# Attention scores of a two-layer decoder trunk: float32 products at depth 64 in two halves of the array, in place of stacked float32r parts

## Chip, cores, metric

The kernel runs on one core of a Trainium2 chip. Its engines are TensorE (PE, with its weight loads PEld), VectorE (DVE), ScalarE (ACT), GpSimd (POOL) and SyncE (SP, which issues most transfers). The metric is the device time of one execution in microseconds.

## What is computed

Two residual layers on x of 512 tokens by 1024 channels, float32. Layer 0 mixes tokens by stick-breaking attention (16 heads of 64), layer 1 by dilated window attention (three groups of 8 heads of 64, merged by their softmax denominators). Each is followed by a feed-forward part with a causal convolution of width 3. Cut to what matters here:

```python
# layer 0, per head and block of 128 queries
z = einsum(q, k) * 64 ** -0.5                       # float32
log_not = where(key < query, log_sigmoid(-z), 0)
between = reverse_cumsum(log_not) - log_not
a = where(key < query, exp(log_sigmoid(z) + between), 0)
o = a @ v                                           # then o @ w_o
# layer 1, per group (window, dilation) in ((128, 1), (512, 4), (2048, 16))
s = einsum(q, k) * 64 ** -0.5 + bias(distance)      # inside the window, causal
p = softmax(s);  o_g = p @ v;  o = sum_g softmax(lse)_g * o_g
# after each: x += post_norm(...); x += post_norm(conv_ffn(pre_norm(x)))
```

## The kernel before

Most products run in three passes of float32r: an operand is cast to a high part H, and the rest is a low part L; H by H, H by L and L by H are added (`mm3`, lines 200 to 203). Weights come in chunks of 128 by 1024 through the class `Weights`. `load` issues the transfer, `split` makes H on ScalarE (line 73) and L on VectorE, or on the engine that it is given (line 74), and `done` is called after the last use of a chunk, splits the next and loads one more. Five split chunks are held.

Layer 0 (lines 370 to 583) works on eight pairs of heads. `fill_qk(p)` projects a pair's queries and keys in two chunks, each in two halves of the depth, and yields after each half: four ticks of twelve products of 512 columns per pair. Each chunk ends with `ws.done(nc.gpsimd)`, so the split of the next goes to GpSimd, and with `stack` (lines 347 to 367): VectorE scales the product by 1 / rms of the tokens into a temporary f (line 351). For queries, ScalarE casts one head's half to H (357), VectorE makes L beside it (358). For keys, ScalarE casts H twice (362, 363), VectorE makes L (364) and copies it (367). With H of q above L of q on the 128 partitions, and H or L of k twice, two float32r products of depth 128 make a score.

`scores(p, i)` is for query tile i. It makes the scores of two heads (line 468; 512, 384, 256 and 128 keys for i = 0 to 3), adds the mask (472), takes two sigmoids on ScalarE (476, 477), a running product on VectorE (the scan, 479) and the product b * u (482). Tiles 0 and 1 use one bank of PSUM per head; tiles 2 and 3 hold both heads in one bank, and are masked and taken through the sigmoids for both heads at once. `turn_a(p, j)` transposes on TensorE (498) and evicts on VectorE and ScalarE (503, 507, 508). `values(p)` multiplies by v (517), the two heads in two column halves of the array.

The fillers, the projections of the pairs and then products with the output weights (`fill_o`), set the order: at fixed ticks after them stand the parts of each pair. A pair's scores 0 and 1 are queued behind the first half of the next pair's queries, scores 2 and 3 one tick later, and its last transposes just ahead of the scores 0 and 1 of the next pair:

```python
for dt, f, a in (
    (0, scores, 0), (0, scores, 1), (1, scores, 2), (1, scores, 3),
    (2, turn_a, 0), (3, turn_a, 1), (4, turn_a, 2), (4, turn_a, 3),
):
    at_tick(b + dt, f, p, a)          # b = 4 * p + 5
at_tick(b + 5, values, p)
```

All semaphores, and the order within an engine where the data leave it open, come from the tile framework, which also hands out the eight banks of PSUM.

Layer 1 works on four pairs of heads. Group 0 has its scores by `stack` as above (line 840). Groups 1 and 2 have float32 products of depth 64 and 32 by 128 outputs, at eight places of the array (line 847: two row halves by four column quarters); their queries and keys are scaled only (line 824).

Of the kernel before, what the change touches and what calls it, by code (L numbers as in the profile page):

```python
# [10 lines left out]
F32 = mybir.dt.float32  # L11
F32R = mybir.dt.float32r
# [5 lines left out]
P = 128  # L18
# [21 lines left out]
# Columns of one head's bias table: two key blocks of group 0, then groups 1 and 2.  # L40
# [4 lines left out]
class Weights:  # L45
    """The weights in chunks of [128, 1024], in the order of their use: loaded ahead and split
    into the float32r parts H and L, with H + L the weight to 24 bits."""
# [55 lines left out]
def hybrid_trunk_kernel(  # L103
# [39 lines left out]
    # ---- the order of the weights  # L143
# [30 lines left out]
    # The gains of the norms before the sub-layers, by channel.  # L174
# [17 lines left out]
    # The factors 1 / rms by token.  # L192
# [6 lines left out]
    # ---- products in three passes  # L199
# [5 lines left out]
    def proj_f(o, w, k0, k1, cols=slice(0, S)):  # L205
        """128 features by tokens; the chunk holds all of the depth."""
# [4 lines left out]
    def keep_busy(n):  # L211
        """Products that nothing uses: the clock of TensorE rises after some us of work."""
# [30 lines left out]
    def half_sum(ss, b, a, name):  # L243
        """(a + eps + b) / 2"""
# [28 lines left out]
    def fill_rows(ts, sums, idn, name):  # L273
        """1 / rms of a run of token tiles, in `rows` and one token to a partition."""
# [15 lines left out]
    def post_norm(t, m0, ss0, m1, g, name, last):  # L290
        """m0 has been multiplied by the gain."""
# [18 lines left out]
    class Sub:  # L310
        """The end of a sub-layer: its columns in two halves, the second token tile by token
        tile, each followed by the norms that lead to the next sub-layer."""
# [20 lines left out]
        def square(self, t):  # L333
# [3 lines left out]
            # The token tile waits in DRAM for the sub-layer's end; its place serves it.  # L337
# [721 lines left out]
```

## Time and profile before

| | |
|---|---|
| median of 3 runs | 1335.27 us (1334.65 to 1335.76) |
| span of the profiled execution, first to last instruction | 1333.9 us |
| TensorE busy | 1282.0 us, 96% |
| weight loads | 1045.4 us, 78% |
| VectorE busy | 846.1 us, 63% |
| ScalarE busy | 577.1 us, 43% |
| GpSimd busy | 92.8 us, 7% |
| mean granted TensorE clock | 0.982 of full speed |

The profiled execution's own time is its span, 1333.9 us, and what lies around it at the launch; the runs' median is 1.4 us above the span. Matmuls are pipelined, so each one's time in the trace is longer than the distance to the next, and a busy TensorE is not one at its peak. Shares of the whole span mix stages with different limits. A line such as L74 is line 74 of the kernel.

### The profile page before, as it was taken

The page shows a single profiled execution, that of the slowest core. Times are in us where ns is not written, and L with a number is a line of the kernel's source. Part 1 is how long each engine was busy: PE and PEld are TensorE (multiplying, and loading weights), DVE is VectorE, ACT ScalarE, POOL GpSimd, SP SyncE. Part 2 cuts the span into 40 slices and gives each one's busy share as a digit, 9 for nine tenths or more (in the row PEclk, how much of TensorE's full clock was granted, in tenths as well). Part 3 has the DMA queues.
Part 4 walks back from the last instruction along what each step waited for, and adds up shares of the span by engine and source line. Part 5 has one row for each costly group of instructions (what it writes and reads, how often), then busy time and mean ns, then how long its engine had stood idle before and what let it go on. Part 6 is the DMA issues. An engine that isn't in the chain of part 4 may idle for free.

```text
span 1333.9 us, 17026 instructions
## 1 busy us (share of the span) xinstructions
PE 1282.0 (96%) x6568; PEld 1045.4 (78%) x6568; DVE 846.1 (63%) x1485; ACT 577.1 (43%) x949; POOL 92.8 (7%) x101
## 2 busy tenths in 40 slices
PE   8989898989999999999998999999899999999997
PEld 7866666779888888888866888887698888888886
DVE  5289999677777777423573465674877777773224
ACT  6355555446444444222364443454554444442210
POOL 2032222020000000000210000000200000000000
PEclk8999999999999999999998999999899999999999
DMA  5321112233332233333245253332333333333321
GB/s 205 111 79 38 47 43 95 67 127 119 102 95 95 95 95 128 128 100 96 94 154 115 86 133 86 99 103 75 114 111 96 96 98 104 98 127 126 95 64 63
DMA packets 48464, 133.48 MB, mean 100 GB/s; under 512 B 14239, under 2 KB 16319, under 8 KB 48384
## 3 DMA queue, kind: packets, MB, share of 16 engines
q1 hardware_dynamic: 44176, 118.26, 28.2%
q0 software_dynamic: 4208, 14.14, 3.5%
q8 instruction: 51, 0.84, 0.3%
q14 instruction: 29, 0.24, 0.1%
HBM read 122.78 MB, written 9.60 MB: 99 GB/s over the span
## 4 chain that ended last, share of the span: by engine, by line
PE 76%; DVE 12%; issue 6%; ACT 3%; DMA 2%; POOL 0%; SPq 0%; DVEq 0%; ACTq 0%; POOLq 0%
PE up L201 12%; PE up L202 12%; PE up L203 12%; PE dn L202 6%; PE dn L201 6%; PE dn L203 6%; PE dqk L201 4%; DVE u L479 3%; PE dqk L203 3%; PE dqk L202 3%; DVE b L482 3%; DMA wraw<-in_dl_qk_dram 2%; PE v L203 1%; PE v L202 1%; PE v L201 1%
## 5 line engine op out<-in xcount | busy, mean ns | idle before, releaser
L74 DVE TENSOR_TENSOR wl<-wraw,wh 128x1024 fp32r<-128x1024 f32 x175 | 214.1, 1224 | 207.1 <-ACT wh L73 204.6
L73 ACT CAST wh<-wraw 128x1024 fp32r<-128x1024 f32 x204 | 214.4, 1051 | 267.4 <-PE dn L203 137.8
L201 PE MATMUL up<-hH,wh 128*128 128x512 f32 (+1 forms) x768 | 284.9, 375 | 9.8 <-ACT hH L267 9.8
L202 PE MATMUL up<-hL,wh 128*128 128x512 f32 (+1 forms) x768 | 286.1, 374 | 0.0
L203 PE MATMUL up<-hH,wl 128*128 128x512 f32 (+1 forms) x768 | 285.4, 373 | 0.0
L201 PEld LDWEIGHTS up<-hH,wh 128*128 128x128 f32 x768 | 144.6, 190 | 35.7 <-ACT hH L267 10.3
L202 PEld LDWEIGHTS up<-hL,wh 128*128 128x128 f32 x768 | 145.9, 190 | 25.0 <-DVE hL L268 0.3
L203 PEld LDWEIGHTS up<-hH,wl 128*128 128x128 f32 x768 | 145.8, 190 | 24.9
L202 PE MATMUL dn<-wl,gH 128*128 128x512 f32 x352 | 138.7, 394 | 0.0
L201 PE MATMUL dn<-wh,gH 128*128 128x512 f32 x352 | 138.0, 392 | 0.0
L203 PE MATMUL dn<-wh,gL 128*128 128x512 f32 x352 | 136.6, 388 | 0.0
L607 DVE SCALAR_TENSOR_TENSOR up<-work,cw,up 128x510 f32<-128x510 f32 (+1 forms) x176 | 131.4, 751 | 5.0 <-ACT up L605 2.2
L604 DVE TENSOR_TENSOR work<-up,rows 128x512 f32<-128x512 f32 x88 | 60.1, 687 | 70.6 <-PE up L203 70.3
L201 PEld LDWEIGHTS dn<-wh,gH 128*128 128x128 f32 x352 | 66.1, 188 | 15.4
L74 POOL TENSOR_TENSOR wl<-wraw,wh 128x1024 fp32r<-128x1024 f32 x29 | 71.5, 2472 | 95.0 <-ACT wh L73 94.7
L201 PE MATMUL dqk<-hH,wh 128*128 128x512 f32 x192 | 77.8, 405 | 0.0
L203 PEld LDWEIGHTS dn<-wh,gL 128*128 128x128 f32 x352 | 66.1, 188 | 14.8
L202 PEld LDWEIGHTS dn<-wl,gH 128*128 128x128 f32 x352 | 66.2, 188 | 13.1
L203 PE MATMUL dqk<-hH,wl 128*128 128x512 f32 x192 | 75.1, 391 | 0.0
L202 PE MATMUL dqk<-hL,wh 128*128 128x512 f32 x192 | 75.0, 391 | 0.0
L605 ACT ACTIVATE up<-work,cb,cw 128x512 f32<-128x512 f32 x88 | 68.5, 779 | 11.3 <-DVE work L604 10.9
L618 ACT CAST gH<-work 128x512 fp32r<-128x512 f32 x44 | 27.2, 619 | 106.6 <-DVE work L617 106.6
(251 smaller groups left out, 1897.3 us busy)
## 6 DMA issues: line engine op xcount, KB each, us to landing
wraw<-in_up_dram SPq DMA_DIRECT2D x88, 512.0 KB, 3.5
wraw<-in_down_dram SPq DMA_DIRECT2D x44, 512.0 KB, 3.5
wraw<-in_dl_qk_dram SPq DMA_DIRECT2D x24, 512.0 KB, 3.6
wraw<-in_sb_qk_dram SPq DMA_DIRECT2D x16, 512.0 KB, 3.5
wraw<-in_dl_v_dram SPq DMA_DIRECT2D x12, 512.0 KB, 3.6
wraw<-in_sb_v_dram SPq DMA_DIRECT2D x8, 512.0 KB, 4.2
wraw<-in_sb_o_dram SPq DMA_DIRECT2D x8, 512.0 KB, 3.4
x<-x_away POOLq DMA_DIRECT2D x8, 512.0 KB, 3.6
```

The costliest lines, as they stand in the source:

```text
L73: nc.scalar.copy(h, raw)
L74: (engine or nc.vector).tensor_tensor(low, raw, h[:].bitcast(F32), op=ALU.subtract)
L201: nc.tensor.matmul(o, sH, mH, start=first, stop=False)
L202: nc.tensor.matmul(o, sH, mL, start=False, stop=False)
L203: nc.tensor.matmul(o, sL, mH, start=False, stop=last)
L479: nc.vector.tensor_tensor_scan(u[:, h, 1:], u[:, h, 1:], zeros[:, : w - 1], 1.0, op0=ALU.mult, op1=ALU.add)
L482: nc.vector.tensor_tensor(b, b, u, op=ALU.mult)
L604: nc.vector.tensor_tensor(h, o, rows, op=ALU.mult)
L605: nc.scalar.activation(o, h, AF.Identity, bias=cb[:, f : f + 1], scale=cw[:, f, 2:3])
L607: nc.vector.scalar_tensor_tensor(o[:, : S - s], h[:, s:], cw[:, f, 2 - s : 3 - s], o[:, : S - s], op0=ALU.mult, op1=ALU.add,)
L618: nc.scalar.copy(gH[:, f, :], u)
```

## The change

In both layers, the queries and keys of a pair are only scaled, into one float32 tile for queries and keys (`scaled`), and the scores of the two heads are float32 products of depth 64, one head in the upper and one in the lower half of the array's rows, each into its own bank (`two_heads`). `stack` is gone, with its casts, differences and copies. In layer 0 the splits after a projection go to VectorE (`ws.done()`), all evictions of the transposed weights go to ScalarE, every query tile has a bank per head and masks and sigmoids by head, b has two buffers for each query tile, and u and b of tiles 2 and 3 leave the shared temporaries. The qk tiles rotate over three places instead of two sets of three. In layer 1 the qk tiles of all three groups alternate between two sets of places. The diff also drops comments.

```diff
-    def stack(o, which, q, kh, kl, scale, name):
-        f = temp(f"f{name}{which}")
+    def scaled(o, which, qk, scale):
         nc.vector.scalar_tensor_tensor(
-            f, o, 1.0 if which else scale, rows, op0=ALU.mult, op1=ALU.mult
+            qk[which], o, 1.0 if which else scale, rows, op0=ALU.mult, op1=ALU.mult
         )
+    def two_heads(outs, lhs, rhs):
         for h in range(2):
-            r, r2 = (slice(n * HD, n * HD + HD) for n in (h, 1 - h))
-            if which == 0:
-                nc.scalar.copy(q[r, h, :], f[r, :])
-                nc.vector.tensor_tensor(
-                    q[r2, h, :], f[r, :], q[r, h, :].bitcast(F32), op=ALU.subtract
-                )
-            else:
-                nc.scalar.copy(kh[r, h, :], f[r, :])
-                nc.scalar.copy(kh[r2, h, :], f[r, :])
-                nc.vector.tensor_tensor(
-                    kl[r, h, :], f[r, :], kh[r, h, :].bitcast(F32), op=ALU.subtract
-                )
-                nc.vector.tensor_copy(kl[r2, h, :], kl[r, h, :].bitcast(F32))
+            r = slice(h * HD, h * HD + HD)
+            nc.tensor.matmul(outs[h], lhs[r, :], rhs[r, :], start=True, stop=True,
+                             tile_position=(h * HD, 0))
...
         def fill_qk(p):
-            q, kh, kl = (parts(p, n) for n in range(3))
-            qk[p] = (q, kh, kl)
+            t = xp.tile([P, 2, S], F32, name=f"qk{p}", tag=f"x{p % 3}")
+            qk[p] = [t[:, n, :] for n in range(2)]
             for which in range(2):
...
-                ws.done(nc.gpsimd)
-                stack(o, which, q, kh, kl, HD**-0.5, f"{p}")
+                ws.done()
+                scaled(o, which, qk[p], HD**-0.5)
                 yield
...
         def scores(p, i):
-            q, kh, kl = qk[p]
+            q, k = qk[p]
             w = S - i * P
-            pool = ap if i < 2 else tp
-            u, b = (
-                pool.tile([P, 2, w], F32, name=f"{n}{p}{i}", tag=f"{n}{i}" if i < 2 else "temp")
-                for n in "ub"
-            )
+            u = ap.tile([P, 2, w], F32, name=f"u{p}{i}", tag=f"u{i}")
+            b = ap.tile([P, 2, w], F32, name=f"b{p}{i}", tag=f"b{i}", bufs=2)
             nc.gpsimd.memset(u[:, :, 0:1], 1.0)
-            if i < 2:
-                zs = [(bank(f"z{p}{i}{h}")[:, :w].unsqueeze(1), slice(h, h + 1)) for h in range(2)]
-            else:
-                o = bank(f"z{p}{i}")
-                zs = [(o[:, : 2 * w].rearrange("p (h w) -> p h w", h=2), slice(0, 2))]
-            for z, hs in zs:
-                for n, h in enumerate(range(hs.start, hs.stop)):
-                    for k in (kh, kl):
-                        nc.tensor.matmul(z[:, n, :], q[:, h, i * P : (i + 1) * P],
-                                         k[:, h, i * P :], start=k is kh, stop=k is kl)
...
+            zs = [bank(f"z{p}{i}{h}")[:, :w] for h in range(2)]
+            two_heads(zs, q[:, i * P : (i + 1) * P], k[:, i * P :])
+            for h, z in enumerate(zs):
+                nc.vector.tensor_tensor(z[:, :P], z[:, :P], mask, op=ALU.add)
+                nc.scalar.activation(u[:, h, 1:], z[:, : w - 1], AF.Sigmoid, scale=-1.0)
+                nc.scalar.activation(b[:, h, :], z, AF.Sigmoid)
...
             if w <= 256:
-                nc.vector.tensor_copy(
+                nc.scalar.copy(
                     at[:, :, c0 : c0 + w], o[:, : 2 * w].rearrange("p (h w) -> p h w", h=2)
                 )
             else:
-                nc.vector.tensor_copy(at[:, 0, c0 : c0 + w], os[0])
-                nc.scalar.copy(at[:, 1, c0 : c0 + w], os[1])
+                for h in range(2):
+                    nc.scalar.copy(at[:, h, c0 : c0 + w], os[h])
...
         def fill_qk(hp):
...
+                if hp % 2:
+                    t = qp.tile([P, 2, S], F32, name=f"dqk{hp}{g}", tag=f"q{g}", bufs=1)
                 else:
-                    t = xp.tile([P, 2, S], F32, name=f"dqk2{hp}", tag="x3")
-                    qk[hp, g] = [t[:, n, :] for n in range(2)]
+                    t = xp.tile([P, 2, S], F32, name=f"dqk{hp}{g}", tag=f"x{g}")
+                qk[hp, g] = [t[:, n, :] for n in range(2)]
...
         def scores(hp, i):
...
-            for h in range(2):
-                for k in (kh, kl):
-                    nc.tensor.matmul(zs[h][:, 2 * P : (2 + nb) * P], q0[:, h, i * P : (i + 1) * P],
-                                     k[:, h, i * P : (i + nb) * P], start=k is kh, stop=k is kl)
+            two_heads([z[:, 2 * P : (2 + nb) * P] for z in zs], q0[:, i * P : (i + 1) * P],
+                      k0[:, i * P : (i + nb) * P])
```

## Rows read from the trace of the kernel before

**Rows 1.** Windows: stretch, its length, busy us of PE, PEld, DVE, ACT, POOL, PEclk, DMA, GB/s.
```profile
78.88:237.82 158.94, 139.00 (x673) 103.38 (x673) 151.34 (x214) 86.39 (x160) 37.98 (x44) 0.95 0.17 56
237.82:254.42 16.60, 16.60 (x93) 12.88 (x93) 14.03 (x25) 8.11 (x16) 0.00 (x0) 1.00 0.22 69
767.00:930.00 163.00, 162.25 (x1355) 131.16 (x1354) 97.57 (x287) 75.57 (x138) 2.18 (x4) 1.00 0.35 101
```
**Rows 2.** Waits, 78.88 to 237.82: who waited for whom, total us, times, longest.
```profile
PE z L468 <- ACT qk L363: 9.7, 12, 1.1
PE ta L498 <- DVE b L482: 9.6, 8, 1.8
```
**Rows 3.** Timeline of PE, pair 0's first scores, last pair's round: start, us, what.
```profile
75.13 0.39 PE L468 MATMUL z<-qk,qk 128*128 128x512 f32 x1
77.00 2.04 PE L468 MATMUL z<-qk,qk 128*128 128x512 f32 x7 [1.48 <-DVE qk L367]
...
237.82 0.40 PE L201 MATMUL o<-wh,oH 128*128 128x512 f32 x1
...
240.68 2.37 PE L517 MATMUL o<-at,v_sb 128*64 128x512 f32 x16
242.98 1.14 PE L468 MATMUL z<-qk,qk 128*128 128x256 f32 x8
243.95 0.44 PE L201 MATMUL o<-wh,oH 128*128 128x512 f32 x1
...
254.42 0.48 PE L201 MATMUL o<-wh,oH 128*128 128x512 f32 x1
```
**Rows 4.** Timeline of DVE and POOL: a split beside scans, and scans alone.
```profile
128.37 3.93 DVE L479 TENSOR_TENSOR_SCAN u<-u,spare 128x383 f32<-128x383 f32 x2
...
128.74 2.74 POOL L74 TENSOR_TENSOR wl<-wraw,wh 128x1024 fp32r<-128x1024 f32 x1
...
242.44 1.79 DVE L479 TENSOR_TENSOR_SCAN u<-u,spare 128x383 f32<-128x383 f32 x2
```
**Rows 5.** Windows, tile u alone: length, busy us of DVE, ACT, POOL, then as above.
```profile
78.88:237.82 158.94, 90.25 (x84) 22.40 (x42) 2.12 (x30) 0.95 0.17 56
237.82:254.42 16.60, 9.14 (x12) 3.25 (x6) 0.00 (x0) 1.00 0.22 69
```
**Rows 6.** Windows, tile qk alone: length, busy us of PE, PEld, DVE, ACT.
```profile
78.88:237.82 158.94, 111.11 (x437) 80.91 (x436) 35.29 (x56) 25.95 (x42) 0.95 0.17 56
```
**Rows 7.** Windows, tile at alone, columns as in the group before.
```profile
78.88:237.82 158.94, 14.25 (x96) 6.35 (x96) 15.48 (x28) 6.64 (x14) 0.95 0.17 56
```
**Rows 8.** Lines by form: count, busy us, mean ns, idle before and what ended it.
```profile
L73 ACT CAST wh<-wraw 128x1024 fp32r<-128x1024 f32 x204 | 214.4, 1051 | 267.4 <-PE dn L203 137.8 <-PE up L202 59.8 <-PE dqk L202 34.0
L74 DVE TENSOR_TENSOR wl<-wraw,wh 128x1024 fp32r<-128x1024 f32 x175 | 214.1, 1224 | 207.1 <-ACT wh L73 204.6
...
L351 DVE SCALAR_TENSOR_TENSOR f<-qk,rows 128x512 f32<-128x512 f32 x16 | 10.7, 671 | 2.1 <-PE qk L203 2.1
...
L507 DVE COPY at<-ta 128x512 f32<-128x512 f32 x8 | 5.4, 677 | 0.0
...
L508 ACT COPY at<-ta 128x512 f32<-128x512 f32 x8 | 4.6, 579 | 0.1
```
**Rows 9.** Timeline of PE, dilated scores of one query tile.
```profile
781.88 0.63 PE L840 MATMUL dz<-dqk,dqk 128*128 128x256 f32 x4
782.44 0.34 PE L847 MATMUL dz<-dqk,dqk 64*32 64x128 f32 x8
782.44 0.45 PE L847 MATMUL dz<-dqk,dqk 64*32 64x128 f32 x16
782.68 0.42 PE L847 MATMUL dz<-dqk 64*32 64x128 f32 x16
783.04 0.50 PE L201 MATMUL dqk<-hH,wh 128*128 128x512 f32 x1
```
**Rows 10.** Timeline of PE, nine transposes in a row.
```profile
116.46 1.15 PE L498 MATMUL ta<-ident,b 128*128 128x128 f32 x9
```

More of the change, by code (lines that the diff above doesn't have):

```diff
@@ L417, in hybrid_trunk_kernel @@
                                              AF.Copy, scale=r_in[u])
-        spare = [xp.tile([P, D], F32, name="spare3", tag="x3")]
-        zeros, mask = spare[0][:, :S], spare[0][:, S : S + P]
-        nc.gpsimd.memset(spare[0], 0.0)
+        spare = xp.tile([P, D], F32, name="spare3", tag="x3")
+        zeros, mask = spare[:, :S], spare[:, S : S + P]
+        nc.gpsimd.memset(spare, 0.0)
         nc.gpsimd.affine_select(
@@ L428, in hybrid_trunk_kernel @@
         qk = {}
-        def parts(p, n):
-            if p % 2 == 0:
-                return xp.tile([P, 2, S], F32R, name=f"qk{p}{n}", tag=f"x{n}")
-            return qp.tile([P, 2, S], F32R, name=f"qk{p}{n}", tag=f"qk{n}")
         def fill_qk(p):
-            q, kh, kl = (parts(p, n) for n in range(3))
-            qk[p] = (q, kh, kl)
+            t = xp.tile([P, 2, S], F32, name=f"qk{p}", tag=f"x{p % 3}")
+            qk[p] = [t[:, n, :] for n in range(2)]
             for which in range(2):
@@ L451, in scores @@
         def scores(p, i):
-            q, kh, kl = qk[p]
+            q, k = qk[p]
             w = S - i * P
-            pool = ap if i < 2 else tp
-            u, b = (
-                pool.tile([P, 2, w], F32, name=f"{n}{p}{i}", tag=f"{n}{i}" if i < 2 else "temp")
-                for n in "ub"
-            )
-            nc.gpsimd.memset(u[:, :, 0:1], 1.0)
-            if i < 2:
-                zs = [(bank(f"z{p}{i}{h}")[:, :w].unsqueeze(1), slice(h, h + 1)) for h in range(2)]
-            else:
-                o = bank(f"z{p}{i}")
-                zs = [(o[:, : 2 * w].rearrange("p (h w) -> p h w", h=2), slice(0, 2))]
-            for z, hs in zs:
-                for n, h in enumerate(range(hs.start, hs.stop)):
-                    for k in (kh, kl):
-                        nc.tensor.matmul(z[:, n, :], q[:, h, i * P : (i + 1) * P],
-                                         k[:, h, i * P :], start=k is kh, stop=k is kl)
-            for z, hs in zs:
-                nh = hs.stop - hs.start
-                nc.vector.tensor_tensor(
-                    z[:, :, :P], z[:, :, :P], mask.unsqueeze(1).broadcast_to([P, nh, P]),
-                    op=ALU.add,
-                )
-                nc.scalar.activation(u[:, hs, 1:], z[:, :, : w - 1], AF.Sigmoid, scale=-1.0)
-                nc.scalar.activation(b[:, hs, :], z, AF.Sigmoid)
+            u = ap.tile([P, 2, w], F32, name=f"u{p}{i}", tag=f"u{i}")
+            b = ap.tile([P, 2, w], F32, name=f"b{p}{i}", tag=f"b{i}", bufs=2)
+            nc.gpsimd.memset(u[:, :, 0:1], 1.0)
+            zs = [bank(f"z{p}{i}{h}")[:, :w] for h in range(2)]
[4 more added lines that the diff above has]
+                nc.scalar.activation(b[:, h, :], z, AF.Sigmoid)
             for h in range(2):
@@ L801, in fill_qk @@
             for g in range(DG):
-                if g == 0:
-                    pool, tag = (qp, "q") if hp % 2 else (xp, "x")
-                    qk[hp, g] = [
-                        pool.tile([P, 2, S], F32R, name=f"dqk{hp}{n}", tag=f"{tag}{n}", bufs=1)
-                        for n in range(3)
-                    ]
-                elif g == 1:
-                    qk[hp, g] = [qp.tile([P, S], F32, name=f"dqk1{hp}{n}", tag=f"g1{n}")
-                                 for n in range(2)]
-                else:
-                    t = xp.tile([P, 2, S], F32, name=f"dqk2{hp}", tag="x3")
-                    qk[hp, g] = [t[:, n, :] for n in range(2)]
+                if hp % 2:
+                    t = qp.tile([P, 2, S], F32, name=f"dqk{hp}{g}", tag=f"q{g}", bufs=1)
+                else:
+                    t = xp.tile([P, 2, S], F32, name=f"dqk{hp}{g}", tag=f"x{g}")
+                qk[hp, g] = [t[:, n, :] for n in range(2)]
                 for which in range(2):
@@ L820, in fill_qk @@
                     ws.done()
-                    if g == 0:
-                        stack(o, which, *qk[hp, g], -(HD**-0.5), f"d{hp}")
-                    else:
-                        nc.vector.scalar_tensor_tensor(
-                            qk[hp, g][which], o, 1.0 if which else -(HD**-0.5), rows,
-                            op0=ALU.mult, op1=ALU.mult,
-                        )
+                    scaled(o, which, qk[hp, g], -(HD**-0.5))
                     yield
@@ L834, in scores @@
             nb = 2 if i < NT - 1 else 1
-            q0, kh, kl = qk[hp, 0]
+            q0, k0 = qk[hp, 0]
             zs = [bank(f"dz{hp}{h}{i}") for h in range(2)]
             z4s = [z[:].rearrange("p (s k) -> p s k", s=4) for z in zs]
-            for h in range(2):
-                for k in (kh, kl):
-                    nc.tensor.matmul(zs[h][:, 2 * P : (2 + nb) * P], q0[:, h, i * P : (i + 1) * P],
-                                     k[:, h, i * P : (i + nb) * P], start=k is kh, stop=k is kl)
+            two_heads([z[:, 2 * P : (2 + nb) * P] for z in zs], q0[:, i * P : (i + 1) * P],
+                      k0[:, i * P : (i + nb) * P])
             for g in (1, 2):
```

1 line of the change is left out of this document (removed).

## The prediction

> **What bounds the kernel now.** I read the busy time by stage first. Over the whole span TensorE is busy 96%, which hides one stage: the attention of layer 0, between the end of the first score products (78.88 us) and the end of the last early ones (237.82 us). There VectorE is busy 151.34 of 158.94 us, TensorE 139.00, ScalarE 86.39, and TensorE's granted clock falls to 0.95 [rows 1]. These are seven rounds, one for each further pair of heads: 158.94 / 7 = 22.70 us each. The waits of this stretch say who is late: TensorE waits 9.7 us for the casts of the stacked keys and 9.6 us for the last product b<-b,u before the transposes, 2.8 us a round together, and both stand behind VectorE's queue [rows 2].
>
> The same round without most of that load stands in the trace: the last pair, 237.82 to 254.42 us. Its fillers are the output products, as many as two projections have; there is no stacking and GpSimd is idle. TensorE does it in 16.60 us, busy all the time at full clock, with VectorE at 14.03 us [rows 1, 3]. Only the pair's early score products lie outside that stretch. So this stage is bound by VectorE, and TensorE's own work is some 18 us a round.
>
> The dilated layer is another matter: from 767 to 930 us TensorE is busy 162.25 of 163.00 us at full clock, VectorE 97.57 [rows 1]. What is taken from VectorE there is worth nothing; only what the change does to TensorE's own time counts.
>
> **The change part by part.** VectorE first, over the seven rounds.
>
> Stacking. 56 VectorE instructions on the tile qk take 35.29 us [rows 6]. The 14 scalings stay (0.671 us each [rows 8], 9.4 us, now writing qk directly), so 25.9 us go: 3.70 a round. ScalarE's 42 casts of 25.95 us go with them.
>
> Evictions of the transposed weights. 28 VectorE copies into at, 15.48 us [rows 7], move to ScalarE: 2.21 a round off VectorE. On ScalarE the same 512 columns take 0.579 for 0.677 us [rows 8], so about 1.9 a round there.
>
> GpSimd's splits. Each round has two, and while one reads SBUF, VectorE's instructions with two SBUF inputs stand still: two scans of 383 columns take 3.93 us beside a GpSimd split of 2.74, and 1.79 us where GpSimd is idle [rows 4]. Over all scans and products into u and b, the seven rounds take 90.25 us, against 9.14 us for the twelve of the undisturbed pair [rows 5]: 90.25 - 7 x 9.14 = 26.3 us, 3.75 a round. This goes with the splits. The splits themselves come to VectorE at 1.224 us [rows 8]: +2.45 a round.
>
> Masks. The two narrow query tiles are masked head by head, two instructions of 128 columns more: +0.4, between nothing and a third of a scan of 383 columns (0.9) each. Sum for VectorE: (151.34 - 25.9 - 15.48 - 26.3) / 7 + 2.45 + 0.4 = 14.8 us a round. ScalarE: 12.3 - 3.7 + 1.9 = 10.5, and four sigmoids more, each under the 0.58 of a 512-column copy: below 12.9 us. Neither reaches TensorE's 18.
>
> TensorE. No score product of this kind (float32, 64 rows by 128 columns) is in the trace. The nearest rows are two. The value products are float32, with the two heads in two column halves; a pair's eight cover 512, 384, 256 and 128 columns for each head, just what a pair's scores cover, and take 2.30 us from start to the next engine work (240.68 to 242.98) [rows 3]. And the dilated products of groups 1 and 2 are float32 with 64 rows in both row halves: eight start together (the first two rows at 782.44 are a narrow and a wide cut of the same stretch), and 32 parts of 128 columns take 0.60 us (782.44 to 783.04) [rows 9], where one such part takes 0.11 us by itself (nine transposes of 128 columns in 1.15 us [rows 10]). Four column quarters alone would need 8 x 0.11 = 0.88, so the row halves overlap. A pair's scores therefore cost between 2.3 us (halves side by side) and 4.6 (one after the other); I take 2.3, plus 0.3 because they come in two bursts, each with its change of array shape. Of the old cost only the late burst, 0.97 us (242.98 to 243.95), lies in the 16.60 [rows 3]. TensorE's round: 16.60 - 0.97 + 2.6 = 18.2, say 18.3 us.
>
> The array's change of shape, into a burst and out of it, is what the old products didn't pay. The rows put both ways together at 0.1 to 0.2 us: 2.30 against 20 parts of 0.11 for one head's 1280 columns, and 0.60 against 4 x 0.11 [rows 3, 9, 10]. I have 0.2 for each of the two bursts, 0.1 in the 2.30 and 0.3 on top. The Trainium skill ("TensorEngine Tiling (Array Packing)", Key Properties) speaks against the edit here: changing the tiling mode drains TensorE, so each burst would pay for its entry and its exit. It gives no price; by a drain of twice what these rows show, the sum would be 0.4 us a round or 2.8 us in all higher, 1308.7, which I count inside the forecast.
>
> Waits that stay. In the last pair TensorE waited for nothing [rows 1]; now it waits 2.8 us a round. After the change VectorE has 3.5 us of slack, so I stay near the first end and take 0.4, for evictions that queue before the sigmoids on ScalarE and for eight score banks a round instead of six. Late next would be the scaled keys: they follow the last projection by a cast (1.05), a split (1.22) and the scaling (0.67) [rows 8], while TensorE has half of the next projection to do, (16.60 - 2.30 - 0.97 - 20 x 0.11) / 4 = 2.8 us, and 14 transposes, 1.5. That cover is just enough as long as VectorE isn't behind.
>
> First scores. Before, the burst of pair 0 runs from 75.13 to 78.88 with a wait of 1.48 us for stacked keys [rows 1, 3]. New: 896 of the 1280 columns, 1.6, plus 0.2: 1.9 us saved.
>
> Dilated layer. Four products of 256 columns take 0.56 us (781.88 to 782.44) [rows 9]; the new pair by the price above 2.30 x 256 / 1280 = 0.46 plus a change of shape, 0.1 to 0.2. That is 0 to +0.1 on 16 tiles; I take +0.5 us in all. If the halves don't overlap it is +0.4 each, +6 us. The stacking removed there lies beside a full TensorE and is worth nothing; so is the other placing of the qk tiles, which can free a buffer earlier but not shorten a full TensorE.
>
> The other stages keep their work; what follows 254.42 only starts earlier.
>
> Sum: 7 x (22.70 - 18.3 - 0.4) = 28.0, + 1.9, - 0.5 = 29.4 us less. The profiled span is 1333.9 us and the median of the runs 1335.27, 1.4 us around the span. 1333.9 - 29.4 + 1.4 = 1305.9 us.
>
> **The rivals.** (a) The two halves run one after the other. For it: the only rows of float32 in row halves have narrow 32-column parts. Against it: eight of those start together. The round would be 18.3 + 2.3 = 20.6, the first burst 0.3 us shorter than now instead of 1.9, the dilated layer 6 us longer: 7 x (22.70 - 20.6 - 0.4) + 0.3 - 6 = 6.2 us saved, 1329.1.
>
> (b) Waits remain. VectorE is in order, and score tiles, banks and moved evictions still make a chain through two engines; if two thirds of the present 2.8 us stay, the round is 20.2: 7 x 2.5 + 1.9 - 0.5 = 18.9 saved, 1316.4. For it: half of the new work on ScalarE stands ahead of sigmoids that VectorE needs. Against it: VectorE's slack of 3.5 us.
>
> (c) Slower. A split on VectorE waits for its cast, and the cast for the last product that reads the old chunk. If it stands at the head of VectorE's queue ahead of scans, everything behind it waits. VectorE reaches today's round at (22.70 - 14.8) / 2 = 4.0 us of waiting for each split; at 5 the time would be 1335.3 + 7 x 1.9 - 1.9 = 1347. Against it: VectorE's 175 splits elsewhere wait 204.6 us for casts, 1.2 us each [rows 8], which makes 14.8 + 2.3 = 17.1 and stays under 18.3.
>
> **Chances.** Forecast 0.73, (b) 0.13, (a) 0.07, (c) 0.04, no difference because two of them add up 0.03. Changes under 0.2% (2.7 us) can't be told from none; so faster 0.93, same 0.03, slower 0.04. The range goes from 1301, the sum with no waits left and no cost in the dilated layer (1302.6) less the uncertainty of 0.2 us in TensorE's round, to 1319, which takes in (b); (a), (c) and no difference are left out, 0.14.
>
> **What would show it.** Rounds of 18 to 19 us with VectorE under 85% busy and the clock at 1.0 in that stage. Score products of the two heads starting within some 10 ns of each other, 0.43 us apart part by part at 512 columns: if the second head starts when the first ends, (a) is right. Scans of 383 columns at 0.95 us throughout. A dilated layer of unchanged length. TensorE's waits in the stage well under 5 us in all; if the largest is for scaled keys or for b, (b) is right; long idle time of VectorE ahead of its splits, ended by a cast, is (c). Wrong outright would be a dilated layer that grows by more than 3 us, or TensorE filling a round of over 20 us without waiting.

## The result and the profile after

The changed kernel takes 1300.56 us (median, 1300.04 to 1304.9), the kernel before, on the same chip, 1334.96 us (1334.42 to 1335.76): a ratio of 0.9747, 95% interval 0.9733 to 0.9762. That is 34.4 us less. The prediction was 1305.9 us with a range of 1301 to 1319; the time lies 5.3 us under the one and 0.4 us under the low end of the other.

The head of the page of the changed kernel's profile:

```profile
span 1298.9 us, 16927 instructions
PE 1267.5 (98%) x6568; PEld 1027.6 (79%) x6568; DVE 776.0 (60%) x1413; ACT 552.3 (43%) x941; POOL 53.1 (4%) x85
```

The windows of the changed kernel, with the columns of [rows 1]. They run from the end of pair 0's first score burst to the end of the last early one, in three cuts (the first round, five rounds, the last round), then comes the last pair:

```profile
76.06:92.29 16.23, 16.23 (x87) 12.40 (x85) 14.14 (x25) 10.24 (x25) 0.41 (x4) 1.00 0.19 58
92.29:184.75 92.46, 92.46 (x502) 67.28 (x500) 73.40 (x125) 55.58 (x126) 2.05 (x20) 1.00 0.20 67
184.75:200.46 15.71, 15.71 (x90) 11.25 (x88) 14.69 (x25) 11.01 (x26) 0.41 (x4) 1.00 0.18 68
200.46:219.11 18.65, 17.32 (x95) 12.96 (x93) 12.22 (x21) 9.61 (x22) 0.00 (x0) 1.00 0.38 114
```

In the five full rounds TensorE has no gap at all: 92.46 of 92.46 us busy, clock at 1.00, 18.49 us a round. VectorE is at 73.40 / 5 = 14.68 us a round, 79%, ScalarE at 11.1. The first round lacks value products, since no pair stands ahead of it, and the last lacks half a projection, since the filler there yields before its first product: 87 and 90 products against 502 / 5 = 100. The whole stretch takes 200.46 - 76.06 = 124.40 us against 158.94 [rows 1].

The waits of the changed kernel from 76.06 to 219.2 us (who waited for whom; total us, times, longest), VectorE's largest and the only one of TensorE:

```profile
DVE z L445 <- PE z L358: 17.6, 7, 3.2
...
PE z L358 <- DVE z L445: 1.3, 1, 1.3
```

Beside [rows 2] the order has turned round: TensorE waited 19.3 us for casts and b, and now VectorE waits 2.5 us a round for TensorE's scores.

The timeline of TensorE in the changed kernel: pair 0's first scores, a late and an early burst inside the rounds, the last pair, and one query tile of the dilated layer:

```profile
74.36 1.77 PE L358 MATMUL z<-qk 64*128 64x512 f32 x8
76.06 0.50 PE L201 MATMUL qk<-hH,wh 128*128 128x512 f32 x1
...
97.53 0.92 PE L358 MATMUL z<-qk 64*128 64x256 f32 x8
98.39 0.50 PE L201 MATMUL qk<-hH,wh 128*128 128x512 f32 x1
...
181.43 1.69 PE L468 MATMUL ta<-ident,b 128*128 128x128 f32 x14
183.05 1.77 PE L358 MATMUL z<-qk 64*128 64x512 f32 x8
184.75 0.50 PE L201 MATMUL qk<-hH,wh 128*128 128x512 f32 x1
...
205.74 0.92 PE L358 MATMUL z<-qk 64*128 64x256 f32 x6
206.59 0.51 PE L201 MATMUL o<-wh,oH 128*128 128x512 f32 x1
...
208.65 0.48 PE L358 MATMUL z<-qk 64*128 64x128 f32 x2 [1.33 <-DVE z L445]
...
746.22 0.70 PE L358 MATMUL dz<-dqk 64*128 64x256 f32 x4
746.86 0.67 PE L802 MATMUL dz<-dqk 64*32 64x128 f32 x32
```

Start to next start, a pair's scores take 1.70 us (183.05 to 184.75) and 0.86 us (97.53 to 98.39): 2.56 us. The first burst, 3.75 us before with its wait [rows 1, 3], takes 1.70. The last pair has a wait that it didn't have. The dilated tile's four products take 0.64 us (0.56 in [rows 9]).

A burst also costs something outside itself. In the changed kernel the 14 transposes ahead of an early burst take 1.62 us to its start (181.43 to 183.05). In the kernel before, ahead of full-array products, the same 14 take 1.45 us (252.97 to 254.42 [rows 3]):

```profile
252.97 1.69 PE L498 MATMUL ta<-ident,b 128*128 128x128 f32 x14
```

The timeline of TensorE again, cut to the start of the early burst (183.04 to 183.06 us) and then to two narrow stretches behind it; each row takes in all instructions of its kind that run in the cut, and gives the start of the first:

```profile
183.05 0.70 PE L358 MATMUL z<-qk 64*128 64x512 f32 x2
...
183.58 0.92 PE L358 MATMUL z<-qk 64*128 64x512 f32 x4
...
184.01 0.81 PE L358 MATMUL z<-qk 64*128 64x384 f32 x4
```

Two instructions have started by 183.06 us: both heads at once. A float32 product shows as two instructions per head; the second follows 0.53 us after the first, the next tile's 0.43 us after that.

The timeline of VectorE in one round (the row that answers to [rows 4]), and below it the windows of the tiles u, qk and at alone over the five rounds, with the columns of [rows 5 to 7]:

```profile
170.55 1.79 DVE L449 TENSOR_TENSOR_SCAN u<-u,spare 128x383 f32<-128x383 f32 x2
```

```profile
92.29:184.75 92.46, 47.15 (x60) 17.46 (x41) 2.05 (x20) 1.00 0.20 67
92.29:184.75 92.46, 73.03 (x322) 50.42 (x320) 6.74 (x10) 1.00 0.20 67
92.29:184.75 92.46, 11.88 (x80) 5.33 (x80) 13.99 (x30) 1.00 0.20 67
```

Tile u: 47.15 / 5 = 9.43 us of VectorE a round, against 90.25 / 7 = 12.9 before and 9.14 in the undisturbed pair [rows 5]; two scans of 383 columns take 1.79 us. Tile qk (PE, PEld, DVE): only the ten scalings are left on VectorE, 1.35 us a round. Tile at (PE, PEld, ACT): VectorE has none, ScalarE 2.80 us a round.

By its stages, the 35.0 us between the two spans are: seven rounds 158.94 - 124.40 = +34.5, first scores +2.05, the last pair 16.60 - 18.65 = -2.05, all that comes ahead of the first scores +0.77 (75.13 to 74.36), all that follows the last pair's last transposes -0.3 (1079.5 to 1079.8 us).

### The profile page after: what moved, and what is told of

It reads as the page before. It is cut to its first block, busy times and chain, and to the rows that moved or that the text cites. A ratio compares the mean times of both kernels' runs of the same rounds, so it can differ in the third digit from the quotient of the medians.

```text
span 1298.9 us, 16927 instructions
## 1 busy us (share of the span) xinstructions
PE 1267.5 (98%) x6568; PEld 1027.6 (79%) x6568; DVE 776.0 (60%) x1413; ACT 552.3 (43%) x941; POOL 53.1 (4%) x85
## 3 DMA queue, kind: packets, MB, share of 16 engines
q1 hardware_dynamic: 44176, 118.26, 29.4%
## 4 chain that ended last, share of the span: by engine, by line
PE 88%; issue 5%; DVE 3%; DMA 3%; ACT 1%; POOL 0%; SPq 0%; DVEq 0%; ACTq 0%; POOLq 0%
PE up L201 13%; PE up L202 12%; PE up L203 12%; PE dn L202 6%; PE dn L201 6%; PE dn L203 6%; PE dqk L201 4%; PE dqk L203 3%; PE dqk L202 3%; PE qk L201 2%; PE qk L203 2%; PE qk L202 2%; DMA wraw<-in_dl_qk_dram 2%; PE z L358 1%; PE v L203 1%
## 5 line engine op out<-in xcount | busy, mean ns | idle before, releaser
L74 DVE TENSOR_TENSOR wl<-wraw,wh 128x1024 fp32r<-128x1024 f32 x191 | 233.6, 1224 | 213.8 <-ACT wh L73 211.2
L203 PEld LDWEIGHTS dn<-wh,gL 128*128 128x128 f32 x352 | 66.1, 188 | 14.8
L586 ACT ACTIVATE work<-up 128x512 f32<-128x512 f32 x44 | 26.3, 597 | 73.3 <-DVE up L577 73.3
```

The lines of the kernel that those rows point to most:

```text
L74: (engine or nc.vector).tensor_tensor(low, raw, h[:].bitcast(F32), op=ALU.subtract)
L203: nc.tensor.matmul(o, sL, mH, start=False, stop=last)
L586: nc.scalar.activation(g, og, AF.Silu)
```

## The experiments

The theory: the rounds were bound by VectorE's sum, and are now bound by TensorE's; so a round takes whichever is longer. The rivals: it was a late step (the stacked keys) and not the sum that cost the time; or one of the three edits (stacks, GpSimd's splits, evictions) made the whole gain. "Round" below is the distance between the early bursts of two pairs, taken over full rounds only, and every kernel is timed against the kernel before on its own chip.

**The splits back on GpSimd** (e1_splits_gpsimd), in the changed kernel:

```diff
-                ws.done()
+                ws.done(nc.gpsimd)
```

> The changed kernel with the 16 splits of layer 0's projections back on GpSimd. Theory (VectorE was the bound, TensorE is now): VectorE's round of 14.7 us loses 2.4 of splits and gains up to 3.75 of standing still, 16.0 at most, under TensorE's 18.5: 1300 to 1303 us, and VectorE's time on tile u back near 90 us. Rival (the collisions with GpSimd were what made the rounds late, wherever VectorE's sum stood): each of the two collisions delays a chain by 1.5 to 2 us a round, 1310 to 1325 us.

1303.23 us (1301.02 to 1304.62), ratio 0.9748 (0.973 to 0.9767): no difference that can be told. Windows of five rounds, all engines, then tile u alone (DVE, ACT, POOL):

```profile
90.60:183.06 92.46, 92.46 (x501) 67.28 (x500) 69.87 (x115) 55.33 (x126) 30.68 (x31) 1.00 0.20 63
90.60:183.06 92.46, 54.92 (x60) 17.51 (x40) 2.02 (x20) 1.00 0.20 63
```

The rounds are 18.49 us as before the edit. Tile u takes 54.92 - 47.15 = 7.8 us more, so the collision is there, but at 1.55 us a round, not the 3.75 that I had read (the last section shows where it falls); and without the splits VectorE's sum is even lower, 14.0. Under a full TensorE neither matters.

**The splits on VectorE, in the kernel before, alone** (e2_before_splits_vector): the reverse edit in the old `fill_qk`, nothing else of the change.

> The kernel before with only those splits moved from GpSimd to VectorE. Theory: VectorE's 21.6 us a round lose 3.75 of standing still and gain 2.45 of splits, 20.3, with about 1 us of waits as before 21.4: seven rounds save 9 us, about 1326 us. Rival (collisions alone were the bound): most of the 34 us, under 1310. Rival (a split at the head of VectorE's queue waits for its cast): no gain or slower, over 1335.

1321.62 us (1321.01 to 1322.61), ratio 0.9888 (0.9873 to 0.9903). Windows of four rounds, all engines, then tile u:

```profile
112.60:198.04 85.44, 78.29 (x400) 59.97 (x401) 81.91 (x135) 50.38 (x93) 1.04 (x16) 0.96 0.16 50
112.60:198.04 85.44, 36.97 (x48) 13.05 (x24) 1.04 (x16) 0.96 0.16 50
```

Alone, the same one-line edit saves 14.0 us, more than the 9 that I expected. VectorE stays full (20.5 of 21.36 us a round, 96%), and tile u falls to 9.24 us a round: in the old kernel the collision did cost what it was priced at.

**The evictions back on VectorE** (e3_evict_vector), in the changed kernel:

```diff
-                nc.scalar.copy(
+                nc.vector.tensor_copy(
...
-                for h in range(2):
-                    nc.scalar.copy(at[:, h, c0 : c0 + w], os[h])
+                nc.vector.tensor_copy(at[:, 0, c0 : c0 + w], os[0])
+                nc.scalar.copy(at[:, 1, c0 : c0 + w], os[1])
```

> The changed kernel with the evictions of the transposed weights placed as before (two of three columns sets on VectorE). Theory: VectorE 14.7 + 2.2 = 16.9 us a round, still under 18.5: 1300 to 1303 us. Rival (VectorE's slack is smaller than its sum says, because it waits for ScalarE within a pair): 1305 to 1312 us.

1305.21 us (1304.53 to 1307.16), ratio 0.9767 (0.9751 to 0.9783). Windows of five rounds, and the last pair's wait in the timeline of TensorE:

```profile
90.94:183.53 92.59, 92.59 (x501) 67.40 (x501) 85.17 (x148) 48.23 (x105) 2.03 (x20) 1.00 0.21 63
```

```profile
210.67 0.48 PE L358 MATMUL z<-qk 64*128 64x128 f32 x2 [2.83 <-DVE z L445]
```

VectorE at 17.0 us a round, 92%, still doesn't lengthen a round (18.52). The time itself lies above the 1303 that I expected, where I had put the rival, that VectorE's slack is smaller than its sum says; the ratio's interval overlaps with that of the changed kernel. What the profile shows of a loss, 3.2 us in the stage, is nearly all in the last pair: its wait grows from 1.33 to 2.83 us, and the clock falls behind it. So the rival holds there and not in the rounds.

**Both back** (e4_both_back): the two edits above together. What is left of the change in layer 0 is the end of the stacks, with the bank per head and the second buffers.

> The changed kernel with splits on GpSimd and evictions as before, so that only the score products and the stacking differ from the kernel before. Theory: VectorE 14.7 - 2.4 + 3.75 + 2.2 = 18.2 us a round, about as much as TensorE's 18.5, so waits of 0.5 to 1.5 us a round: 1304 to 1311 us. Rival (the stacked parts were the whole of it, the rest is free): 1300 to 1302. Rival (the scores are the small part): over 1318.

1304.04 us (1301.69 to 1305.6), ratio 0.975 (0.9731 to 0.9769).

```profile
91.97:184.43 92.46, 92.46 (x501) 67.29 (x500) 81.21 (x137) 47.71 (x105) 30.85 (x31) 1.00 0.20 63
```

The rounds are 18.49 us with VectorE at 16.2, 88%. I had expected 18.2 and waits of 0.5 to 1.5 us a round; the waits didn't come, since the collision is 1.55 us here too and not 3.75. The end of the stacks, with the banks and buffers that came with it, brings the rounds to TensorE's bound by itself. What the banks and buffers give without it, no run shows.

**The stacks kept** (e6_stacks_kept): the converse; the splits, evictions, banks per head are as in the changed kernel, layer 0's scores again float32r products of stacked parts. For room, b of each tile has one buffer and the narrowest tile lies in the shared temporaries.

```diff
-                scaled(o, which, qk[p], HD**-0.5)
+                stack(o, which, *qk[p], HD**-0.5, f"{p}")
...
-            two_heads(zs, q[:, i * P : (i + 1) * P], k[:, i * P :])
+            for h, z in enumerate(zs):
+                for k in (kh, kl):
+                    nc.tensor.matmul(z, q[:, h, i * P : (i + 1) * P], k[:, h, i * P :],
+                                     start=k is kh, stop=k is kl)
```

> The changed kernel with layer 0's scores by stacked float32r parts as before; splits on VectorE, evictions on ScalarE and a bank for each head stay (b has one buffer, and the narrowest query tile lies in the shared temporaries, for space). Theory: VectorE 14.7 + 3.3 = 18.0 us a round, and keys that come late through cast, difference and copy: rounds of 19 to 20.5 us, 1304 to 1316 us. Rival (float32 scores save TensorE time): the round is longer by that saving even where TensorE waits for nothing, visible as score bursts over 1.70 and 0.86 us. Rival (stacking is harmless once GpSimd and the evictions are out of the way): 1300 to 1302 us.

1314.17 us (1313.12 to 1314.87), ratio 0.9848 (0.9831 to 0.9864). Windows of three rounds, and TensorE's only wait in them:

```profile
132.08:191.18 59.10, 57.05 (x302) 43.30 (x301) 55.82 (x94) 42.54 (x94) 1.00 (x12) 1.00 0.17 54
```

```profile
PE z L467 <- DVE qk L373: 2.0, 6, 0.4
```

Rounds of 19.70 us, VectorE at 18.6, 94% (the two full rounds ahead of these three take 21.50 us, at a clock of 0.92, and 18.90). So the other edits alone, with b in one buffer, give 20.3 us; with the stacks gone they give nothing more that can be told (e4). What TensorE still waits for is the last copy of the stacked keys. The timeline of TensorE, the first early burst of these rounds:

```profile
132.08 0.50 PE L467 MATMUL z<-qk,qk 128*128 128x512 f32 x1
...
135.20 0.40 PE L201 MATMUL qk<-hH,wh 128*128 128x512 f32 x1
```

The burst takes 3.12 us for 1.70 in the changed kernel. That is more than the 1.21 us by which the round is longer, so here all of the difference stands where the products follow the copy. The late step and a VectorE at 94% come together in this kernel, and it can't tell them apart. The expectation's other rival, that float32 products save TensorE time, is met by e7 below: in the dilated layer, which TensorE fills, the stacked products are the shorter ones.

**Every score product twice** (e5_scores_twice): the same products again into the same banks.

```diff
-            two_heads(zs, q[:, i * P : (i + 1) * P], k[:, i * P :])
+            for _ in range(2):
+                two_heads(zs, q[:, i * P : (i + 1) * P], k[:, i * P :])
```

> The changed kernel with every score product of layer 0 made twice into the same bank. Theory: TensorE is the bound there, so each round grows by the burst's passes without its change of shape, 2.13 us: 8 x 2.1 = 17 us, about 1317. Rival (TensorE has room in these rounds): less than 8 us. If the two heads ran one after the other it would be 34 us.

1318.6 us (1318.16 and 1319.03), ratio 0.9883 (0.9864 to 0.9903).

```profile
93.02:196.58 103.56, 103.56 (x581) 74.22 (x580) 75.32 (x125) 53.98 (x126) 2.02 (x20) 1.00 0.19 59
```

Rounds of 20.71 us: all of the added 2.22 us lands in the round. TensorE is the bound, and a second pass costs 2.22 us. The first costs a round more: without its late burst the last pair of the kernel before took 16.60 - 0.97 = 15.63 us [rows 1, 3], so the two bursts bring 18.49 - 15.63 = 2.86. The difference, 0.64 us a round or 0.32 a burst, is the change of shape: 0.34 of it within the bursts (2.56 - 2.22), 0.17 in the transposes ahead of the early one, and the rest in the twelve products behind each, 2.94 and 2.87 us for 2.86 and 2.82 in the kernel before.

**Load on VectorE, untied** (e9_load_2 and e10_load_5): two or five additions of 512 columns after each scaling, of a tile of zeros into a temporary that nobody reads.

```diff
                 scaled(o, which, qk[p], HD**-0.5)
+                for _ in range(5):
+                    nc.vector.tensor_tensor(temp(f'load{p}{which}'), zeros, zeros, op=ALU.add)
```

> The changed kernel with four idle additions of 512 columns more a round on VectorE (two after each scaling, of 0.6 to 0.7 us), whose result nothing uses. Theory: VectorE 14.7 + 2.6 = 17.3 us, under TensorE's 18.5: within 2 us of 1300.6. Rival (hidden waits eat the slack): over 1305.

> The same with ten additions a round. Theory: VectorE 14.7 + 6.3 = 21.0 us becomes the bound again, rounds of 21 to 22 us, 8 rounds x 2.5 to 3.5: 1318 to 1328 us. Rival (VectorE was never the bound, the waits were latency of the stacking): under 1308.

1302.1 us (ratio 0.976, 0.9699 to 0.9822) and 1307.87 us (0.9803, 0.9753 to 0.9854). The additions wait for no data, and most ran ahead of the rounds that they were meant for: all 32 of e9 start between 29.3 and 52.7 us, so e9 says nothing of the rounds, and the 80 of e10 between 29.8 and 131.1 us. Within two full rounds of e10 run 13 and 9 of them. Windows of e10, these two and the three without load:

```profile
90.66:112.81 22.15, 19.10 (x101) 13.52 (x101) 22.09 (x39) 11.40 (x27) 0.41 (x4) 1.00 0.15 48
112.81:132.93 20.12, 20.12 (x101) 14.25 (x101) 20.01 (x35) 9.91 (x24) 0.41 (x4) 0.92 0.15 52
132.93:188.41 55.48, 55.48 (x302) 40.38 (x301) 44.93 (x76) 33.36 (x76) 1.23 (x12) 1.00 0.23 71
```

The time, 1307.87, lies where I had put the rival, that VectorE was never the bound; the rounds speak against it. With VectorE busy for over 99% they take 22.15 and 20.12 us, and without the load 55.48 / 3 = 18.49.

**Load on VectorE, tied** (e11_load_tied): the same five additions, each reading the tile just scaled, so that none can run early.

```diff
                 scaled(o, which, qk[p], HD**-0.5)
+                for _ in range(5):
+                    nc.vector.tensor_tensor(temp(f'load{p}{which}'), qk[p][which], zeros, op=ALU.add)
```

> The changed kernel with five more additions of 512 columns on VectorE behind each scaling of a qk tile, each reading the tile just scaled, so that they fall into every round: ten a round of about 0.69 us, none of their results used. If VectorE's sum of 20.5 us was what bound the rounds of the kernel before, its 14.7 us of the changed kernel and 6.5 to 6.9 us of load make 21.2 to 21.6, VectorE is busy for nearly all of each round, the rounds go from 18.5 to 21 to 22 us and the time to 1318 to 1328. If instead the stacked parts cost the time as a late step in the chain from the projection to the scores, and VectorE's fullness only came with it, the load is taken up by its slack and the time stays under 1308.

1326.77 us (1326.11 to 1331.28), ratio 0.9945 (0.9928 to 0.9962). Windows of the first and of the other four of the five full rounds, and TensorE's largest wait within the five:

```profile
92.88:117.98 25.10, 25.10 (x104) 16.35 (x103) 21.96 (x38) 11.13 (x26) 0.41 (x4) 0.78 0.17 52
117.98:200.41 82.43, 76.87 (x402) 54.95 (x401) 79.65 (x137) 42.78 (x101) 1.64 (x16) 0.98 0.16 55
```

```profile
PE qk L201 <- DVE oL L345: 5.4, 3, 2.5
```

Rounds of 107.53 / 5 = 21.51 us on average, VectorE at 20.3, 94%. The first of them has no wait: TensorE is busy for all of its 25.10 us at a clock of 0.78, behind a wait of 2.82 us for b that ends at 90.59. The other four take 20.61 us each, with VectorE at 19.9, 97%, and TensorE waits for results of VectorE, hardly for b as in [rows 2] (0.2 us in the five rounds) but for the low part of the outputs (oL). There is no stack in this kernel: a full VectorE alone takes a round from 18.49 to 20.6 us, and with the clock that falls behind the waits 26.2 of the 34.4 us are gone again. So the sum is enough to lengthen the rounds, without the late step, though some of it may be the place of the additions, which stand in VectorE's queue five at a time. The step isn't nothing: in e6 the stacked keys are what TensorE waits for last, 0.7 us of idle time a round in a burst that is 1.4 us longer.

**The dilated layer's group 0 stacked again** (e7_dilated_stacked): `stack`, the two float32r products and the old placing of the qk tiles there only, layer 0 as changed.

```diff
-                    scaled(o, which, qk[hp, g], -(HD**-0.5))
+                    if g == 0:
+                        stack(o, which, *qk[hp, g], -(HD**-0.5), f"d{hp}")
+                    else:
+                        scaled(o, which, qk[hp, g], -(HD**-0.5))
```

> The changed kernel with group 0 of the dilated layer by stacked float32r parts as before, so that only layer 0 is changed. Theory: that layer is TensorE's throughout and the two kinds of product cost nearly the same: 1299.5 to 1301.5 us. Rival (the float32 pair costs more, or the change of array shape does): 1296 to 1299. Rival (the stacking held something back there): 1302 to 1306.

1300.11 us (1298.28 to 1303.24), ratio 0.9747 (0.9729 to 0.9766). The timeline of TensorE, the first tile of the layer:

```profile
745.40 0.63 PE L829 MATMUL dz<-dqk,dqk 128*128 128x256 f32 x4
745.96 0.45 PE L836 MATMUL dz<-dqk,dqk 64*32 64x128 f32 x16
```

0.56 us again in place of 0.64. From the first to the last score product the layer takes 143.77 us against 145.23 in the changed kernel (and 143.76 in the kernel before): 1.46 us, too little to see in the runs. On most tiles, where transposes stand ahead, it is these that become longer. The second tile in the timeline of TensorE, in the kernel before and in the changed one:

```profile
788.66 0.60 PE L885 MATMUL tp<-ident,ds 128*128 128x128 f32 x4
789.01 0.71 PE L840 MATMUL dz<-dqk,dqk 128*128 128x256 f32 x4
```

```profile
753.03 0.60 PE L840 MATMUL tp<-ident,ds 128*128 128x128 f32 x4
753.56 0.70 PE L358 MATMUL dz<-dqk 64*128 64x256 f32 x4
```

The four transposes take 0.53 us to the start of the products for 0.35, and the products then take as long as before (0.63 us to the next start, 0.65 before).

**The last pair's narrowest tile one tick later** (e8_last_pair), against its wait:

```diff
-                at_tick(b + dt, f, p, a)
+                at_tick(b + dt + (p == SBP - 1 and f is scores and a == 3), f, p, a)
```

> The changed kernel with the scores of the last pair's last query tile one tick later, since TensorE stood 1.33 us for a bank of PSUM there. Theory: that wait goes and nothing else moves, 1299.0 to 1299.8 us. Rival (the late tile delays the last transposes or the wait moves to the next bank): 1300.5 or more.

1301.71 us (1298.69 to 1302.89), ratio 0.9753 (0.9736 to 0.9771). In the timeline of TensorE the pair's two narrow tiles start at 204.42 and 208.01 us, each with both heads together and without a wait. From the first score product to the last pair's last transpose it is 143.07 us instead of 144.72. The median doesn't show the 1.65 us.

**Both of these** (e12_both_layers_best):

> The changed kernel with the dilated layer's first group of scores made by stacked parts again (1.46 us shorter in that stage when done alone) and the last query tile of the last pair scored one tick later (1.65 us shorter there when done alone). If the two stages are as steady as their profiles showed them, the two add: about 3.1 us under the changed kernel, 1297.5. If what varies in the other stages from run to run is larger than this, the time can't be told from the changed kernel's, 1299 to 1302.

1299.05 us (1298.24 to 1299.59), ratio 0.9734 (0.9716 to 0.9751), profiled span 1296.6 us. The two stages keep their gains together (143.07 and 143.76 us), so 3.1 us are there in the trace; the median is 1.5 us under that of the changed kernel, with overlapping intervals. It is the lowest median here, and can't be told apart from 1300.56.

The rounds of the kernels in one table, each from its windows shown; for the kernel before, from the window of its five full rounds, with the last of them alone below it:

```profile
97.68:213.19 115.51, 103.64 (x501) 76.83 (x501) 109.58 (x156) 62.42 (x116) 26.95 (x30) 0.94 0.14 46
190.08:213.19 23.11, 19.78 (x101) 14.41 (x101) 21.90 (x32) 12.49 (x24) 5.51 (x6) 1.00 0.14 47
```

| kernel | VectorE, us a round | share | TensorE idle | clock | round, us |
|---|---|---|---|---|---|
| before | 21.9 | 95% | 2.4 | 0.94 | 23.10 |
| e2, before with splits on VectorE | 20.5 | 96% | 1.8 | 0.96 | 21.36 |
| e10, changed, its two rounds with untied load | 21.0 | 99.6% | 1.5 | 1.00, 0.92 | 21.14 |
| e11, changed with tied load | 20.3 | 94% | 1.1 | 0.78, then 0.98 | 21.51 |
| e6, changed with stacks | 18.6 | 94% | 0.7 | 1.00 | 19.70 |
| e3, evictions on VectorE | 17.0 | 92% | 0 | 1.00 | 18.52 |
| e4, splits and evictions back | 16.2 | 88% | 0 | 1.00 | 18.49 |
| changed | 14.7 | 79% | 0 | 1.00 | 18.49 |
| e1, splits on GpSimd | 14.0 | 76% | 0 | 1.00 | 18.49 |
| e5, scores twice | 15.1 | 73% | 0 | 1.00 | 20.71 |

From 18.6 us of VectorE upward, the round follows VectorE's sum, 0.1 to 1.2 us above it; from 17.0 downward it is TensorE's 18.49 to 18.52 (20.71 in e5), whatever VectorE does. In most of the upper rows the clock is lower too, but in the kernel before it doesn't set the round: four of its five rounds have a clock of 0.93 and take 23.09 to 23.12 us, and the last has the full clock and takes 23.11.

## Why the prediction was right, and where its sum was off

**The mechanism held.** VectorE bound the rounds (e2, e10, e11 and the table), the change took it from there, and TensorE's own work became the bound (e5). How much of the old rounds' excess was VectorE's sum and how much the late step of the stacks, the runs don't divide (e6). Two float32 heads in the two row halves run side by side: rival (a) needed the second head to start when the first ends. Rival (b), remaining waits, and (c), a split at the head of VectorE's queue, would show in VectorE-released waits of TensorE: there is one of 1.3 us in the whole stage, and it isn't in a round. VectorE's only idle times ahead of splits that a cast ends, the sign of (c), are two of 5.7 us together, both in the last pair.

**The step that failed is "seven rounds" at one price.** I divided 158.94 us by seven and set 18.3 + 0.4 against each, 130.9 us in all; it was 124.40. The differences:
- The first and the last round are not full. The first has no value products and the last half a projection less: 16.23 + 15.71 instead of 2 x 18.49, -5.0 us. This could have been read before: the early bursts of the old kernel stand 23.10 us apart, not 22.70, and the tick table says which work the edges lack. The low end of my range took in no waits and 0.2 us of TensorE's round, and not this.
- The waits of 0.4 us a round are none: -2.8 us.
- TensorE's round is 18.49, not 18.3: +1.3 us. The passes were priced right (2.22 us by e5, against 2.2), the change of shape too low: 0.32 us a burst against 0.2. The bursts alone take the 2.56 us that the sum has as 2.6, but 0.30 more lies in the products around them, which the sum leaves out.

**VectorE's sum** came out as worked: 14.68 us for 14.8. ScalarE's evictions take 2.80 us a round, as the 6.64 / 7 that it had [rows 7] and the 1.9 that I moved there make.

**The collision with GpSimd** was priced right for the old kernel (e2: 12.9 - 9.24 = 3.65 us a round for 3.75) and was no credit of this change: e4 shows that the two edits that free VectorE further add nothing that can be told once the stacks are gone. Without the stacks 31.6 us (e4), with the other edits alone 20.3 (e6), together 34.4: the gains of edits that unload one engine don't add past the point at which the next engine binds.

**The first scores** gained 2.05 us in the burst for 1.9.

**The last pair** cost 2.05 us, which I had at nothing. By the code, eight banks are held when its last score product comes up: four by the output rows, two by tile 2, one by the values, one by tile 3's first head; its second head needs a ninth. The trace bears this out. The timeline of ScalarE just ahead of that product, which starts at 208.65 us:

```profile
208.22 0.38 ACT L447 ACTIVATE b<-z 128x256 f32<-128x256 f32 x1
```

The wait is put down to VectorE's mask, which ends at 208.64 us, 0.01 us ahead of the start. Where the releaser is plain, TensorE starts 0.05 us behind it (in this trace at 260.33 us, behind a ScalarE result that ends at 260.27). ScalarE's second sigmoid of tile 2's first head, the last reader of that bank, ends at 208.60, just this far ahead. The same 0.01 and 0.05 us stand in e1, e3 and e4. That the place in the order makes the wait is shown by e8, which gets back 1.65 of the 2.05 us.

**The dilated layer** cost 1.47 us for 0.5, near the 1.6 of its upper bound, and for the same reason as the rounds: the sum compared the products alone, and the entry into the new shape stands ahead of them, 0.18 us where transposes come first (0.53 for 0.35, e7).

So the change of shape was priced too low in both layers: 0.1 to 0.2 us by the rows, 0.2 in the sum, 0.32 a burst by e5. The Trainium skill ("TensorEngine Tiling (Array Packing)", Key Properties) says that a change of tiling mode drains TensorE. The trace agrees as far as the early burst pays at its entry and both bursts pay behind. The price, 0.32 us, lies between the 0.2 of the sum and the drain of twice that which the prediction weighed: 18.49 us a round, between 18.3 and 18.7.

The total came near in part by luck: costs that the sum had 7.8 us too high (the edges of the stage, the waits) stand against others that it had 4.4 us too low (the change of shape in both layers, the last pair). The terms close: 6.5 from the rounds, -2.05 from the last pair, +0.15 from the first scores, +0.8 ahead of them, +0.2 behind (the dilated layer's -1.0 lies in it with +1.2 elsewhere) make 5.6 us between the predicted 29.4 and the 35.0 of the spans. The +0.8 and the +1.2 need not be the change's: what it doesn't touch varies as much between profiles (the time to the first scores was 72.8 us in e11 and 74.9 in e12).

## What to carry to other kernels

Price a stage by its full periods and count its edges by themselves: a quotient over all of them hides both the true period and what the edges lack. Price a burst of another array shape by the whole period with and without it: part of what it costs stands in the products ahead of it and behind it. Edits that unload the same engine are worth the way to the next bound once, not each its own price; ask first which of them gets there alone. A load that is to test an engine's slack must read what the stage makes, or it runs ahead of the stage, as all of e9's did.

## What was not expected of the hardware

After the same wait of 1.33 us in the last pair TensorE's clock stayed at full in the changed kernel and fell in e1. The timeline of TensorE in e1 behind the wait, and the windows of that stretch:

```profile
210.24 0.63 PE L202 MATMUL o<-wl,oH 128*128 128x512 f32 x1
210.66 0.63 PE L203 MATMUL o<-wh,oL 128*128 128x512 f32 x1
```

```profile
209.30:212.90 3.60, 3.60 (x10) 2.85 (x10) 2.85 (x8) 1.17 (x6) 0.00 (x0) 0.53 0.51 160
```

The granted clock is 0.53 there, near the lower of its two levels (1.2 of 2.4 GHz), and products that stand 0.23 us apart at full clock stand 0.43 apart; it costs 1.6 us on top of a wait of 1.33. What set the two cases apart, these runs don't show.

The collision of GpSimd's splits with VectorE cost 3.65 us a round where VectorE was full (e2) and 1.55 us where it had slack (e1), with the same two splits a round. The timelines of GpSimd and VectorE in one round of e1:

```profile
152.90 3.15 POOL L74 TENSOR_TENSOR wl<-wraw,wh 128x1024 fp32r<-128x1024 f32 x1 [0.59 <-ACT wh L73]
```

```profile
154.36 2.50 DVE L452 TENSOR_TENSOR b<-b,u 128x768 f32<-128x768 f32 x1
```

The first split meets one product b * u, which takes 2.50 us for 0.95 in the changed kernel (at 172.84 us): that is the whole 1.55. The scans ahead of it (from 152.07 us) keep their 1.79. The second split (161.45 to 163.84 us) slows nothing: VectorE is idle from 161.86 to 165.73 us, waiting for the next scores. In the kernel before, VectorE was 95% busy, and both splits met its work.
